# Gate and up: product 7 of two units as seven half-size products in three groups between the products of the next pair

## The chip, the cores and the metric

One core of a Trainium2 chip runs the whole kernel. The metric is the device time of one execution in microseconds (us), as the median of several runs. A measurement of this kernel is compared with the kernel before on the same chip. The engines are named as in the profile: PE (TensorE, matmuls), PEld (its weight loads), DVE (VectorE), ACT (ScalarE), POOL (GpSimd) and SP (SyncE, which issues DMAs).

## The reference

An encoder trunk of two layers on 1024 tokens of width 1024, in float32. The change concerns the first half of the channel mixer of each layer, the gate-and-up product:

```python
D_FF = 2816
h = rmsnorm(x, norm_ffn[i])
gu = h @ w_gate_up[i]                       # (1024, 1024) @ (1024, 5632)
x = x + (jax.nn.silu(gu[..., :D_FF]) * gu[..., D_FF:]) @ w_down[i]
```

The rest (two kinds of attention, memory heads, output projection, down projection, norms) is as it was.

## The kernel before

A float32 product is made of three fp32r matmuls: each operand is split into a high part (`hi`, L106, a cast on ACT) and a low part (`lo`, L109, a subtraction on DVE), and `three` gives high x high, high x low and low x high, which add up in one bank of PSUM.

Gate and up runs over 22 units a layer (class `Pair`, one for 128 columns of the gate and the 128 of up that belong to them; here the word pair means two such units in a row, u and v, and the pair behind it w and x). The tokens are two halves of 512, and rows of the weights are two halves of 512 too, so that a unit is a 2x2 block product. It is done with seven products instead of eight. Product n (0 to 6) takes a left tile, a sum of blocks of the weight, and a right tile `B[n]`, a sum of blocks of the normalized tokens, kept for the whole layer. A product is 12 matmuls of 128x512 (4 row blocks by 3 terms, L886). Products 0, 2, 4 and 6 go into bank X of the unit (units take turns between two banks), 1, 3 and 5 into Y.

`prepare` makes the left tiles of two products at a time. Products 0 and 1 use the raw weight as loaded; products 2 and 3 use a sum and a difference that POOL forms in the tile `wS` (L848, L841), products 4 and 5 two more differences that POOL writes over the same `wS`; product 6 uses half of the raw tile. The split tiles are `wgu2` for 2 and 3 (one buffer), `wgu6` for 6 (one buffer), `wgu` for the others (three buffers). A `prepare` is called four products ahead (`lead`), and the ones for products 4 and 6 each start the next load of a raw tile (L937, on SP).

`read` takes the results out: ACT copies (L897 to L909), DVE adds and multiplies (L894), ACT does silu (L900, L915). Product 6 is read by DVE as `c1 -= X` and `c1 *= g1`. After product 6 of the second unit, `hand_over` (L1012) makes from the four results of two units the right tiles of the down projection and stores them (L1006).

The order on PE is the order of `product` calls, unit by unit, except that the first four units (`first`) run two by two, while `right_sides` makes the `B` tiles for them step by step on DVE and ACT (L975, L978). The order on the other engines comes from a scheduler, as engines follow the program and the tiles' buffers. At the end of a layer's list the first tiles of the down projection are made ready (L1058 on), and its products follow (L1178).

Of the kernel before, what the change touches and what calls it, by code (L numbers as in the profile page):

```python
# [41 lines left out]
def trunk_kernel(ctx: ExitStack, tc: tile.TileContext, a: dict, out: bass.AP):  # L42
# [62 lines left out]
    def hi(dst, src):  # L105
        nc.scalar.copy(dst, src)  # L106

    def lo(dst, src, h, eng=None):
        (eng or nc.vector).tensor_tensor(dst, src, h.bitcast(F32), op=ALU.subtract)  # L109
# [74 lines left out]
    class Norm:  # L184
# [6 lines left out]
        def add(self, xk, k=None):  # L191

            n = self.n
            self.xs[len(self.xs) if k is None else k] = xk
            sq = temp("sq", n)
            nc.scalar.activation(sq, xk, AF.Square)
            if len(self.xs) > self.summed:
                while self.acc:
                    self.mean(self.acc.pop(0))
                self.mean(sq)  # L200
                return
            self.acc.append(sq)
            if len(self.xs) > 2:
                self.merge()
# [66 lines left out]
    with tc.tile_pool(name="mp", bufs=1, reuse_waits="tile") as mp:  # L271
# [94 lines left out]
    for layer in range(2):  # L366
# [427 lines left out]
        with (  # L794
            tc.tile_pool(name=f"fs{layer}", bufs=1, reuse_waits="tile") as fs,
            tc.tile_pool(name=f"fp{layer}", bufs=1, reuse_waits="tile") as fp,
        ):
            phase[:] = fp, 21, 5
            wide[:] = True, 2

            def pair(src, dst):
# [17 lines left out]
            norms = [Norm(), Norm()]  # L819

            B = [[None] * 4 for _ in range(7)]
            def load_x(m, f):
                x[m][f] = temp("x")
                nc.sync.dma_start(x[m][f], (a["x"] if is_a else x_d)[m][:, f * HS : (f + 1) * HS])

            class Pair:
# [6 lines left out]
                def prepare(self, n):  # L833

                    n -= n % 2
                    if n in self.left:
                        return
                    g1, g2 = self.raw[0][:, :HS], self.raw[0][:, HS:]
                    if n > 0:
                        u1, u2 = self.raw[1][:, :HS], self.raw[1][:, HS:]  # L840
                    sub = lambda o, p_, q_: nc.gpsimd.tensor_tensor(o, p_, q_, op=ALU.subtract)  # L841
                    s = self.raw[0]
                    if n == 2:
                        self.s = fs.tile([P, D], F32, tag="S", name="wS", bufs=2)
                    if n in (2, 4):
                        s = self.s
                    if n == 2:
                        nc.gpsimd.tensor_tensor(s[:, HS:], u1, u2, op=ALU.add)  # L848
# [12 lines left out]
                    if n == 6:  # L861
                        hi(w[:, 0, :HS], u2)
                        lo(w[:, 1, :HS], u2, w[:, 0, :HS])
                    else:
                        hi(w[:, 0], s)
                        lo(w[:, 1], s, w[:, 0])
                    self.left[n], self.left[n + 1] = w[:, :, :HS], w[:, :, HS:]
                    if n == 4:
                        self.left[4], self.left[5] = self.left[5], self.left[4]
                    if n > 3 or (n == 0 and 2 <= self.j < first):  # L870
                        load_gu()

                def product(self, n):
                    if n == 0:
                        self.X = (
                            ps_s.tile([P, HS], F32, tag="S", name="X")
                            if self.j % 2
                            else ps_mm.tile([P, HS], F32, tag="mm", name="X")
                        )
                    if n in (1, 3):  # L880
                        self.Y = ps_t.tile([P, HS], F32, tag="T", name="Y")
                    ps, w = (self.Y if n in (1, 3, 5) else self.X), self.left[n]
                    for k in range(4):
                        kw = (w[:, 0, k * P : (k + 1) * P], w[:, 1, k * P : (k + 1) * P])
                        for i, (l, r) in enumerate(three(kw, (B[n][k][:, 0], B[n][k][:, 1]))):
                            nc.tensor.matmul(  # L886
                                ps, l, r, start=n in (0, 1, 3, 6) and k == 0 and i == 0,
                                stop=k == 3 and i == 2, skip_group_check=True,
                            )

                def read(self, n):
                    self.seen.add(n)
                    X, Y = self.X, getattr(self, "Y", None)
                    add = lambda o, p_, q_, op=ALU.add: nc.vector.tensor_tensor(o, p_, q_, op=op)  # L894
                    if n == 0:
                        self.g1 = temp("g1")
                        nc.scalar.copy(self.g1, X)  # L897
                    elif n == 1:
                        add(self.g1, Y, self.g1)
                        nc.scalar.activation(self.g1, self.g1, AF.Silu)  # L900
                    elif n == 2:
                        self.g2 = temp("g2")
                        nc.scalar.copy(self.g2, X)  # L903
                    elif n == 3:
                        self.c2 = temp("c2")
                        nc.scalar.copy(self.c2, Y)  # L906
                    elif n == 4:
                        self.c1 = temp("c1")
                        nc.scalar.copy(self.c1, X)  # L909
                        add(self.c2, self.c2, self.c1)  # L910
                        if 5 in self.seen:
                            add(self.c2, self.c2, self.g2, ALU.mult)
                    elif n == 5:
                        add(self.g2, Y, self.g2)
                        nc.scalar.activation(self.g2, self.g2, AF.Silu)  # L915
# [9 lines left out]
            for j in range(0, first, 2):  # L925
                order += [(u, n) for n in (3, 2, 5, 4, 6) for u in us[j : j + 2]]
# [45 lines left out]
            def right_sides():  # L972
# [24 lines left out]
                for k in range(4):  # L997
                    sub(x[k][1], x[k + 4][1], x[k][1])
                    B[4][k] = pair(x[k][1], h_op(k))
                    yield  # L1000
                for k in range(4):
                    B[6][k] = pair(x[k + 4][0], t_op(k))
                    yield

            def keep(i, p, t):
# [26 lines left out]
            def gate_up():  # L1032
                run_some(rest, 1)
                load_gu()
                for i, (u, n) in enumerate(order):
                    if i + lead < len(order):
                        v, n_ = order[i + lead]
                        v.prepare(n_)
                    u.product(n)
# [4 lines left out]
                    yield u, n  # L1044


            wd = a["w_dn"][layer].rearrange("(p i) r c -> p i r c", i=2)
# [162 lines left out]
            for u, n in gate_up():  # L1210
                if u.j == NF - 1 and n in (2, 3, 4):
                    keep_rows(n - 2)
                    if n > 2:
                        left_side(0, n - 3)
                if u.j == NF - 1 and n in (3, 4, 5):
                    right_side(0, n - 3)
# [127 lines left out]
```

## Time and profile before

| | |
|---|---|
| runs shown | 2156.21, 2150.68, 2151.85 us; median 2151.85 |
| profiled execution | 2155.14 us, span 2153.4 us, mean granted TensorE clock 0.992 |
| matmuls of gate and up | L886, three groups X<-hB, X<-hT and Y<-hB of 1056 with 254.2, 254.2 and 257.0 us busy, and smaller ones |
| POOL, DVE and ACT in the gate-and-up | some 13, 23 and 14 us of every 38.16 us |

In a row of the timeline the first number is the start in us, the second the busy time, then engine, line, operation, output<-inputs by the program's names, shape and count, and in brackets the idle time in front with what ended it. In a row of groups the numbers behind the bar are the busy time in all (us) and the mean of one (ns). In a row of windows the busy time of each engine stands in a stretch, the granted clock of PE (1.00 is full), the share of the DMA engines and GB/s.

### The profile page before, as it was taken

Reading aid. Unit: us, or ns where it says so; the run is one execution under the profiler, and the core shown is the slowest. Engines: PE = TensorE matmul, PEld = TensorE weight load, DVE = VectorE, ACT = ScalarE, POOL = GpSimd, SP = SyncE. Lnnn points to the kernel's source line nnn. Section 1 sums busy time; section 2 is a strip of 40 time slices with the busy share of each in tenths; the row PEclk is TensorE's granted clock in tenths of the full one; section 3 lists DMA queues with packets and bytes.
Section 4 is the critical chain, followed back from the end, with each engine's and each line's share of the span. In section 5 each row is a group of like instructions: output and inputs, shape, how many; then the busy total and the mean of one; then the engine's idle time right before and its main releaser. Section 6 shows DMA issues by size and latency. Waiting matters only on the chain.

```text
span 2153.4 us, 27952 instructions
## 1 busy us (share of the span) xinstructions
PE 2111.0 (98%) x9946; PEld 1744.3 (81%) x9946; DVE 1458.7 (68%) x2314; ACT 1045.2 (49%) x1988; POOL 509.5 (24%) x545
## 2 busy tenths in 40 slices
PE   7999999999999999999999999999999999999997
PEld 6788888778888888888778888887888888888886
DVE  7677787786556565866766666667866665567675
ACT  6577785443333334344466665653433333344442
POOL 0344330333333330000233233203233333300000
PEclk9999999999999999999999999999999999999998
DMA  6321118333323336865332212275133323277662
GB/s 247 100 93 44 37 60 287 124 91 100 113 94 117 98 118 225 298 215 201 105 91 66 78 58 72 86 246 168 58 119 117 98 93 113 93 247 261 203 208 93
DMA packets 120076, 287.22 MB, mean 133 GB/s; under 512 B 12288, under 2 KB 18688, under 8 KB 119936
## 3 DMA queue, kind: packets, MB, share of 16 engines
q1 hardware_dynamic: 112896, 272.57, 38.5%
q10 hardware_dynamic: 7040, 12.85, 1.6%
q8 instruction: 79, 1.29, 0.2%
q14 instruction: 61, 0.50, 0.1%
HBM read 210.40 MB, written 68.94 MB: 130 GB/s over the span
## 4 chain that ended last, share of the span: by engine, by line
PE 75%; issue 13%; DVE 4%; ACT 3%; DMA 2%; POOL 2%; DVEq 0%; SPq 0%; ACTq 0%; POOLq 0%
PE X L886 20%; PE Y L886 16%; PE mm L139 14%; PE po L139 6%; PE X L1178 5%; PE Y L1178 4%; PE S L559 3%; PE O L622 3%; PE pT L602 3%; DMA xr_d<-x 1%; DMA x<-in_x 1%; ACT p L574 1%; POOL wS L841 1%; DVE wgu L109 1%; DVE pl L109 0%
## 5 line engine op out<-in xcount | busy, mean ns | idle before, releaser
L109 DVE TENSOR_TENSOR wgu<-wS,wgu 128x1024 fp32r<-128x1024 f32 x88 | 111.0, 1261 | 255.9 <-ACT wgu L106 255.9
L886 PE MATMUL Y<-hB,wgu 128*128 128x512 f32 x1056 | 257.0, 393 | 0.8 <-ACT c L906 0.8
L886 PE MATMUL X<-hB,wgu 128*128 128x512 f32 x1056 | 254.2, 390 | 1.0 <-ACT g L903 1.0
L886 PE MATMUL X<-hT,wgu 128*128 128x512 f32 x1056 | 254.2, 391 | 0.0
L1178 PE MATMUL X<-hB,wd 128*128 128x512 f32 x1056 | 242.4, 390 | 0.9 <-DVE x L1146 0.9
L886 PEld LDWEIGHTS Y<-hB,wgu 128*128 128x128 f32 x1056 | 198.5, 188 | 44.7 <-ACT c L906 1.6
L886 PEld LDWEIGHTS X<-hB,wgu 128*128 128x128 f32 x1056 | 198.4, 188 | 43.9 <-ACT g L903 1.9
L886 PEld LDWEIGHTS X<-hT,wgu 128*128 128x128 f32 x1056 | 198.5, 188 | 42.8
L1178 PEld LDWEIGHTS X<-hB,wd 128*128 128x128 f32 x1056 | 198.0, 188 | 43.1 <-issue 2.3
L587 POOL TENSOR_SCALAR p<-p,stat 128x384 f32<-128x384 f32 (+1 forms) x256 | 141.0, 570 | 313.2 <-DVE stat L584 212.8
L139 PE MATMUL mm<-hT,wqk 128*128 128x512 f32 x672 | 199.9, 405 | 0.1
L139 PE MATMUL po<-yT,wo 128*128 128x512 f32 x768 | 184.7, 394 | 0.0
L1178 PE MATMUL Y<-hB,wd 128*128 128x512 f32 x792 | 180.4, 389 | 0.0
L1178 PEld LDWEIGHTS Y<-hB,wd 128*128 128x128 f32 x792 | 148.5, 188 | 31.2 <-DVE x L1146 0.5
L139 PEld LDWEIGHTS po<-yT,wo 128*128 128x128 f32 x768 | 142.5, 188 | 29.5 <-issue 1.0
L106 ACT CAST wgu<-wS 128x1024 fp32r<-128x1024 f32 x88 | 92.4, 1050 | 131.3 <-POOL wS L841 108.1
L233 POOL TENSOR_TENSOR nr<-nv,neg_half 128x4 f32<-128x4 f32 (+1 forms) x11 | 11.7, 1063 | 598.5 <-DVE nv L232 598.4
L841 POOL TENSOR_TENSOR wS<-wgu_raw 128x512 f32<-128x512 f32 x44 | 65.9, 1498 | 362.9 <-DVE wgu L109 362.9
L106 ACT CAST hB<-b_raw 128x512 fp32r<-128x512 f32 x154 | 89.4, 618 | 112.0 <-DMA b_raw<-b_d 96.0
L574 ACT ACTIVATE p<-p,stat 128x256 f32<-128x256 f32 (+1 forms) x192 | 112.3, 586 | 52.2 <-DVE stat L570 49.5
L109 DVE TENSOR_TENSOR pl<-pT,ph 128x384 fp32r<-128x384 f32 (+1 forms) x256 | 118.7, 494 | 21.8 <-ACT ph L106 18.8
L109 DVE TENSOR_TENSOR hB<-b_raw,hB 128x512 fp32r<-128x512 f32 x154 | 99.8, 686 | 49.5 <-ACT hB L106 49.3
(161 smaller groups left out, 3924.6 us busy)
## 6 DMA issues: line engine op xcount, KB each, us to landing
wgu_raw<-in_w_gu SPq DMA_DIRECT2D x92, 512.0 KB
wd_raw<-in_w_dn SPq DMA_DIRECT2D x70, 512.0 KB
b_raw<-b_d SPq DMA_DIRECT2D x70, 512.0 KB
b_d<-c SPq DMA_DIRECT2D x88, 256.0 KB
b_d<-t SPq DMA_DIRECT2D x66, 256.0 KB
wo_raw<-in_w_out SPq DMA_DIRECT2D x32, 512.0 KB
x<-in_x SPq DMA_DIRECT2D x32, 256.0 KB
xr_d<-x ACTq DMA_DIRECT2D x32, 256.0 KB
```

The costliest lines, as they stand in the source:

```text
L106: nc.scalar.copy(dst, src)
L109: (eng or nc.vector).tensor_tensor(dst, src, h.bitcast(F32), op=ALU.subtract)
L139: nc.tensor.matmul(ps[:, :n], l, r, start=start and i == 0 and j == 0, stop=stop and i == len(order) - 1 and j == 2,)
L233: nc.gpsimd.tensor_tensor(r[:, :nb], v[:, :nb], neg_half[:, :nb], op=ALU.pow)
L559: nc.tensor.matmul(s_[:, :n], Q[self.h][:, qb * P : (qb + 1) * P], k, start=j == 0, stop=j == 1)
L574: nc.scalar.activation(p[:, :n], p[:, :n], AF.Exp, bias=m1, scale=-1.0, accum_out=s1)
L587: nc.gpsimd.tensor_scalar(p[:, :n], p[:, :n], ri[:, i : i + 1], 1.0, op0=ALU.mult, op1=ALU.mult)
L602: nc.tensor.transpose(tr[:, j * P : (j + 1) * P], p[:, j * P : (j + 1) * P], ident)
L622: nc.tensor.matmul(o[:, c0 : c0 + w * P], self.value(j), t[:, s0 : s0 + w].rearrange("p j q -> p (j q)"), start=j == js[0] and t is self.p ...
L841: sub = lambda o, p_, q_: nc.gpsimd.tensor_tensor(o, p_, q_, op=ALU.subtract)
L886: nc.tensor.matmul(ps, l, r, start=n in (0, 1, 3, 6) and k == 0 and i == 0, stop=k == 3 and i == 2, skip_group_check=True,)
L1178: nc.tensor.matmul(bank, l, r, start=i in (0, 1, 3, 6) and p == 0 and n == 0, stop=p == HF - 1 and n == 2, skip_group_check=True,)
```

## The change

Product 7 of a unit (n = 6) is no longer made in the unit. A new class `Fourth` takes it for two units together: the left side is then 2x2 blocks of half the rows and half the columns, and so is the right side, and it is done with seven products of 6 matmuls of 128x256 (42 in place of 24 of 128x512). The result is added into or taken from `c1` of the two units directly. The seven products come in three groups: A (two, 12 matmuls), B (two, 12) and C (three, 18). They stand between the products of the next pair: A, w0, B, w1, C, w2 and so on; for the last pair of a layer they follow at the end. In the first pair's case (`skip`) A, B and C stand after (u2,3), (u3,3).

- Left tiles: `prepare` of group A makes all of them. POOL forms a sum and three differences of 128x256 in a tile `wS4` (L933, L932), ACT and DVE split into four high and four low parts, `wgu4`, in tiles of 2 KB a partition, of which there are now 24 in place of 21. The tile `wgu6` is gone, and so are product 7's own `hi` and `lo`. Both of the loads that product 6 started are started here.
- Right tiles: three new ones, t2, t3 and t4 (`q4h`), formed in `right_sides` by eight DVE operations of 128x256 with three `hi` and three `lo`.
- Banks: X4 and Y4, one each for all three groups. The reads (L985) are seven DVE operations and two products for a pair; A's are two of 128x256, B's two, C's three.
- `hand_over` comes after C.
- `ahead` is the list in which `prepare` is called; the last units' hooks into the down projection now count items from the end.

```diff
-                    elif n == 6 and self.j >= first:
-                        w = fp.tile([P, 2, HS], F32R, tag="w4", name="wgu6", bufs=1)
...
+                def prepare(self, n):
...
+                    nc.gpsimd.tensor_tensor(s1, r1[:, :h2], r1[:, h2:], op=ALU.add)
+                    sub(s2, s1, r0[:, :h2])
+                    sub(s3, r0[:, :h2], r1[:, :h2])
+                    sub(s4, r0[:, h2:], s2)
...
+                def product(self, n):
...
+                    if n == "A":
+                        self.X = ps_t.tile([P, HS], F32, tag="T", name="X4")
+                        self.Y = ps_o.tile([P, HS], F32, tag="O", name="Y4")
+                        self.part(self.X, 0, a11, b11, start=True)
+                        self.part(self.Y, 0, a12, b21, start=True)
+                    elif n == "B":
+                        self.part(self.X, 0, s2, t2)
+                        self.part(self.Y, h2, s1, t1)
                     else:
-                        add(self.c1, self.c1, X, ALU.subtract)
-                        add(self.c1, self.c1, self.g1, ALU.mult)
+                        self.part(self.X, 0, s3, t3)
+                        self.part(self.Y, h2, s4, b22, stop=True)
+                        self.part(self.X, h2, a22, t4, stop=True)
+
+                def read(self, n):
...
+                    if n == "A":
+                        sub(a.c1[:, low], X[:, low])
+                        sub(a.c1[:, low], Y[:, low])
+                    elif n == "B":
+                        sub(a.c1[:, high], X[:, low])
+                        sub(b.c1[:, high], Y[:, high])
+                    else:
+                        sub(
+                            b.c1.rearrange("p (n c) -> p n c", n=2),
+                            X[:, low].unsqueeze(1).to_broadcast([P, 2, h2]),
+                        )
+                        sub(a.c1[:, high], Y[:, high])
+                        sub(b.c1[:, low], X[:, high], ALU.add)
+                        for u in self.units:
+                            sub(u.c1, u.g1, ALU.mult)
...
-            order += [(u, n) for u in us[first:] for n in range(7)]
+            ahead, before = list(order), []
+            for j in range(0, NF, 2):
...
+                z = Fourth(us[j], us[j + 1])
+                parts4 = [(z, n) for n in "ABC"]
+                ahead += own + parts4[:1]
+
+                skip = 2 if j == 2 else 0
+                order += own[:skip]
+                for i, it in enumerate(own[skip:]):
+                    order += before[i : i + 1] + [it]
+                before = parts4
+            order += before
...
-                    if n == 6 and u.j % 2:
-                        hand_over(u.j // 2, us[u.j - 1], u)
+                    if n == "C":
+                        hand_over(u.units[0].j // 2, *u.units)
```

DVE at the end of a unit in the middle of layer 0, before the change; the unit is v, the names with 6007, 6010 and 6044 are the next unit's (w's) tiles for products 2 to 5, raw_5820 belongs to the unit after it (x).

```order
L109 TENSOR_TENSOR wgu2_6010<-wS_6007,wgu2_6010 128x1024
L894 TENSOR_TENSOR c2_5990<-c2_5990,c1_6004 128x512
L109 TENSOR_TENSOR wgu_6044<-wS_6007,wgu_6044 128x1024
L894 TENSOR_TENSOR g2_5972<-Y_5977,g2_5972 128x512
L109 TENSOR_TENSOR wgu_6098<-wgu_raw_5820,wgu_6098 128x1024
L894 TENSOR_TENSOR c2_5990<-c2_5990,g2_5972 128x512
L894 TENSOR_TENSOR c1_6004<-c1_6004,X_5925 128x512
L109 TENSOR_TENSOR wgu6_6079<-wgu_raw_5785,wgu6_6079 128x512
L894 TENSOR_TENSOR c1_6004<-c1_6004,g1_5938 128x512
```

The same place after the change; c1_5922 is u's and c1_6045 is v's, X4 and Y4 are the banks of the two units' `Fourth`.

```order
L109 TENSOR_TENSOR wgu2_6051<-wS_6048,wgu2_6051 128x1024
L889 TENSOR_TENSOR c2_6031<-c2_6031,c1_6045 128x512
L109 TENSOR_TENSOR wgu_6087<-wS_6048,wgu_6087 128x1024
L889 TENSOR_TENSOR g2_6013<-Y_6018,g2_6013 128x512
L985 TENSOR_TENSOR c1_5922<-c1_5922,X4_6069 128x256
L109 TENSOR_TENSOR wgu_6173<-wgu_raw_5945,wgu_6173 128x1024
L889 TENSOR_TENSOR c2_6031<-c2_6031,g2_6013 128x512
L985 TENSOR_TENSOR c1_5922<-c1_5922,Y4_6070 128x256
L985 TENSOR_TENSOR c1_5922<-c1_5922,X4_6069 128x256
L985 TENSOR_TENSOR c1_6045<-c1_6045,Y4_6070 128x256
```

The first five positions are the same but for the lines' numbers; A's reads of X4 and Y4 stand where, or one place ahead of where, the read of product 6 stood, and B's follow.

PE behind v5, the last product of v, after the change (w0's four rows shown by the first and last; Y_6018 is v's bank, X_6092 w's). Before, product 6 of v stood there (two rows of 6 matmuls into X_5925, 128x512), and w0 behind it.

```order
L881 MATMUL Y_6018<-hB_4758,wgu_5942 128x512 x3
L957 MATMUL X4_6069<-hT8_4854,wgu4_5982 128x256 x2
L957 MATMUL X4_6069<-hT8_4854,wgu4_5983 128x256
L957 MATMUL X4_6069<-hT8_4854,wgu4_5982 128x256 x2
L957 MATMUL X4_6069<-hT8_4854,wgu4_5983 128x256
L957 MATMUL Y4_6070<-hT8_4879,wgu4_5982 128x256 x2
...
L881 MATMUL X_6092<-hB_4210,wgu_6015 128x512 x3
...
L881 MATMUL X_6092<-hB_4339,wgu_6015 128x512 x3
L957 MATMUL X4_6069<-q4h_4906,wgu4_5989 128x256
...
L957 MATMUL Y4_6070<-hT8_4854,wgu4_5989 128x256 x2
```

Group B goes into the banks X4 and Y4 that group A filled, one product of w later.

POOL at the same place after the change; wS_6048 is w's and wS_6205 x's.

```order
L849 TENSOR_TENSOR wS_6048<-wgu_raw_5789 128x512
L842 TENSOR_TENSOR wS_6048<-wS_6048,wgu_raw_5698 128x512
L849 TENSOR_TENSOR wS_6205<-wgu_raw_5997 128x512
L842 TENSOR_TENSOR wS_6205<-wS_6205,wgu_raw_5945 128x512
L842 TENSOR_TENSOR wS_6048<-wgu_raw_5698,wgu_raw_5789 128x512
L842 TENSOR_TENSOR wS_6048<-wgu_raw_5698,wS_6048 128x512
L933 TENSOR_TENSOR wS4_6278<-wgu_raw_5997 128x256
L932 TENSOR_TENSOR wS4_6278<-wgu_raw_5789,wgu_raw_5997 128x256
```

The order of the `wS` operations is that of before (x's first two ahead of w's last two); the four of `wS4` are new behind them, and the raw tile of x is loaded by the `prepare` of the pair's group A rather than by those of products 4 and 6 alone.

More of the change, by code (lines that the diff above doesn't have):

```diff
@@ L821, in trunk_kernel @@
             B = [[None] * 4 for _ in range(7)]
+            fourth = []
             def load_x(m, f):
@@ L886, in product @@
                             nc.tensor.matmul(
-                                ps, l, r, start=n in (0, 1, 3, 6) and k == 0 and i == 0,
+                                ps, l, r, start=n in (0, 1, 3) and k == 0 and i == 0,
                                 stop=k == 3 and i == 2, skip_group_check=True,
@@ L924, in trunk_kernel @@
             order = [(u, n) for u in us[:first] for n in (0, 1)]
-            for j in range(0, first, 2):
-                order += [(u, n) for n in (3, 2, 5, 4, 6) for u in us[j : j + 2]]
-            order += [(u, n) for u in us[first:] for n in range(7)]
+            ahead, before = list(order), []
+            for j in range(0, NF, 2):
+                if j < first:
+                    own = [(u, n) for n in (3, 2, 5, 4) for u in us[j : j + 2]]
+                else:
+                    own = [(u, n) for u in us[j : j + 2] for n in range(6)]
+                z = Fourth(us[j], us[j + 1])
[7 more added lines that the diff above has]
+            order += before
             loads = [(us[j], 0) for j in range(first)] + [(us[0], 1), (us[1], 1)]
@@ L1000, in right_sides @@
                     yield
+                t2, t3, t4 = (temp("q4").rearrange("p (k c) -> p k c", k=2) for _ in range(3))
+                for k in range(2):
+                    top, bottom = x[k + 4][0], x[k + 6][0]
+                    sub(t3[:, k], bottom[:, h2:], top[:, h2:])
+                    sub(top[:, h2:], top[:, h2:], top[:, :h2])
+                    sub(t2[:, k], bottom[:, h2:], top[:, h2:])
+                    sub(t4[:, k], t2[:, k], bottom[:, :h2])
+                    yield
                 for k in range(4):
                     B[6][k] = pair(x[k + 4][0], t_op(k))
+                    yield
+                for t in (t2, t3, t4):
+                    f = [fp.tile([P, 2, h2], F32R, tag="t2k", name="q4h", bufs=24) for _ in range(2)]
+                    hi(f[0], t)
+                    lo(f[1], t, f[0])
+                    fourth.append(f)
                     yield
@@ L1034, in gate_up @@
                 load_gu()
+                ready = lead
                 for i, (u, n) in enumerate(order):
-                    if i + lead < len(order):
-                        v, n_ = order[i + lead]
+                    while n in range(6) and ready < min(ahead.index((u, n)) + lead + 1, len(ahead)):
+                        v, n_ = ahead[ready]
                         v.prepare(n_)
+                        ready += 1
                     u.product(n)
@@ L1041, in gate_up @@
                     run_some(rest, 1 if i < 2 * first else 2)
-                    if n == 6 and u.j % 2:
-                        hand_over(u.j // 2, us[u.j - 1], u)
-                    yield u, n
+                    if n == "C":
+                        hand_over(u.units[0].j // 2, *u.units)
+                    yield i - len(order)
             wd = a["w_dn"][layer].rearrange("(p i) r c -> p i r c", i=2)
@@ L1208, in finish @@
                     nc.scalar.dma_start(out[:2].rearrange("k p t -> p k t")[:, :, at:], first)
[L1210 to L1216, printed above, removed]
+            for to_go in gate_up():
+                if -7 <= to_go <= -5:
+                    keep_rows(to_go + 7)
+                    if to_go > -7:
+                        left_side(0, to_go + 6)
+                if -6 <= to_go <= -4:
+                    right_side(0, to_go + 6)
             norms = [Norm(), Norm() if is_a else Norm(HS, 7)]
```

53 lines of the change are left out of this document (46 added, 7 removed).

## The prediction

> **What bounds the kernel now.** I read the page first, for the share of each engine over the whole span, and then went to the gate-and-up stage by stretches.
>
> ```profile
> span 2153.4 us, 27952 instructions
> PE 2111.0 (98%) x9946; PEld 1744.3 (81%) x9946; DVE 1458.7 (68%) x2314; ACT 1045.2 (49%) x1988; POOL 509.5 (24%) x545
> ```
>
> PE is the bound: all idle time that it has is 42 us. The profiled run took 2155.14 us, of which 1.7 lie outside the span. That is 3.3 us above the median of the runs shown (2151.85); the sum below is made against 2155.14 and shifted by 3.3 at the end. The next view is the busy time in stretches of 38.16 us, in layer 0.
>
> ```profile
> core 0: us, PE busy (x) PEld busy (x) DVE busy (x) ACT busy (x) POOL busy (x), PEclk, DMA share, GB/s
> 597.60:635.76 38.16, 38.16 (x169) 31.57 (x169) 23.13 (x24) 14.04 (x20) 12.77 (x8) 1.00 0.31 104
> ```
>
> A pair of units is 14 products of 12 matmuls: 168 matmuls in 38.16 us, 227.1 ns each, 2.73 a product. PE has no idle time here and the others have much. Every pair that the change alters is therefore bound by PE, unless it gives PE a new wait. What stands between them is a chain of other engines that runs once a unit. Here it is at the end of a unit, in the timelines of PE, DVE and POOL.
>
> ```profile
> start us, us, engine line op out<-in xcount [idle before <-releaser]
> 619.24 2.89 PE L886 MATMUL X<-hB,wgu 128*128 128x512 f32 x12
> 621.97 2.89 PE L886 MATMUL Y<-hB,wgu 128*128 128x512 f32 x12
> 624.69 2.89 PE L886 MATMUL X<-hT,wgu 128*128 128x512 f32 x12
> 627.42 2.89 PE L886 MATMUL X<-hB,wgu 128*128 128x512 f32 x12
> ...
> 621.01 1.23 DVE L109 TENSOR_TENSOR wgu<-wS,wgu 128x1024 fp32r<-128x1024 f32 x1 [3.81 <-ACT wgu L106]
> ...
> 626.42 1.22 DVE L109 TENSOR_TENSOR wgu<-wS,wgu 128x1024 fp32r<-128x1024 f32 x1 [2.26 <-ACT wgu L106]
> 627.56 0.68 DVE L894 TENSOR_TENSOR g<-Y,g 128x512 f32<-128x512 f32 x1
> 628.16 1.22 DVE L109 TENSOR_TENSOR wgu<-wgu_raw,wgu 128x1024 fp32r<-128x1024 f32 x1
> 629.30 1.78 DVE L894 TENSOR_TENSOR c<-c,g 128x512 f32<-128x512 f32 x1
> 631.00 0.68 DVE L894 TENSOR_TENSOR c<-c,X 128x512 f32<-128x512 f32 x1
> ...
> 622.32 1.30 POOL L841 TENSOR_TENSOR wS<-wgu_raw 128x512 f32<-128x512 f32 x1 [8.79 <-DVE wgu L109]
> 623.56 1.74 POOL L841 TENSOR_TENSOR wS<-wgu_raw,wS 128x512 f32<-128x512 f32 x1
> ```
>
> Call t0 the start of the unit's product 4 on PE (619.24). The next unit's left tile wgu2 has one buffer, so its first part waits for product 3 to end, at t0. From there one thing follows the other: the low part on DVE (t0+1.8 to +3.0), two subtractions on POOL over the same tile (+3.1 to +6.1), a cast, and the low part of the next unit's tile for products 4 and 5 (+7.2). Behind it, in DVE's order, stand the add of g2, the low part for the unit after next, the product with g2, and only then the read of product 6, at +11.8. Product 6 had left PE by +8.3, so the read comes 3.4 us late; nothing waits for it, since the next unit's product 0 has another bank. The waits view says that the chain is no accident of one unit:
>
> ```profile
> POOL wS L841 <- DVE wgu L109: 362.9, 44, 15.8
> DVE wgu L109 <- ACT wgu L106: 275.7, 90, 6.1
> ```
>
> **The change, part by part.** *Fewer columns on PE.* Per pair 24 matmuls of 512 columns go and 42 of 256 come. The kernel already has matmuls of this width elsewhere:
>
> ```profile
> 42.77 1.95 PE L139 MATMUL mm<-mhl,wm 128*128 128x256 f32 x15
> L139 PE MATMUL mm<-mhl,wm 128*128 128x256 f32 x15 | 1.9, 281 | 0.0
> ```
>
> Fifteen take 1.95 us with the last one's 0.281, so they start (1.95 - 0.28)/14 = 0.119 us apart. Removed 24 x 0.2271 = 5.45, added 42 x 0.119 = 5.00: 0.45 us less a pair, 22 pairs in two layers, **10.0 us less**. The most that this part could give, at half the wide matmul's pace (0.1136), is 0.68 a pair or 15 us.
>
> [...]
>
> *Reads that PE now waits for.* This is the term that decides the sign. The products of a group go into two banks, X4 and Y4, which the groups A, B and C share. Group B adds into columns that A's read must have left, so B's matmuls wait for A's reads on DVE. On PE after the pair's last product (v5) stand A, the next unit's product 0, and B. Unstalled, counted from t0: v4 to +2.73, v5 to +5.45, A (12 x 0.119 = 1.43) to +6.88, product 0 to +9.61, B's X half (0.71) to +10.32, where B's Y half wants A's second read.
>
> On DVE the second read stands in the same place of the chain that the read of product 6 had: behind the low part of the next w4, the add of g2, A's first read, the low part of x0 and the product with g2. From the rows: w4's low part at +7.18, the add of g2 at +8.32 until about +8.92, A's first read 0.38 until +9.30, the low part 1.14 until +10.44, the product with g2 0.60 to 1.70, and the second read 0.38. The 0.38 is from this group, a quarter the size from PSUM:
>
> ```profile
> 1090.95 0.75 DVE L109 TENSOR_TENSOR V<-vtr,V 128x256 fp32r<-128x256 f32 x2
> L894 DVE TENSOR_TENSOR c<-c,g 128x512 f32<-128x512 f32 x31 | 36.5, 1176 | 0.7 <-ACT g L915 0.7
> L894 DVE TENSOR_TENSOR g<-Y,g 128x512 f32<-128x512 f32 x31 | 21.1, 682 | 0.0
> ```
>
> The c, g product takes 1176 on the mean, 1.78 where POOL runs beside it; undisturbed it should be near the 0.60 from the start of g2's add to the next start (627.56 to 628.16). So the second read ends at +11.4 at best and +12.5 as the chain ran in before: PE waits **1.1 to 2.2 us** at each boundary of two pairs.
>
> There is one more thing ahead in the chain. In the changed program POOL has the two subtractions of the unit after next (x2) in front of those for w4; in before they are in front too, but early. They need a raw tile whose load is now issued later, since the raw tile before it is also read for Fourth's left tiles, whose low parts lie some 6 us before t0 on DVE. A load's way to POOL is in these waits:
>
> ```profile
> 629.03 1.50 POOL L848 TENSOR_TENSOR wS<-wgu_raw 128x512 f32<-128x512 f32 x1 [3.72 <-DMA wgu_raw<-in_w_gu]
> 630.61 1.62 POOL L841 TENSOR_TENSOR wS<-wS,wgu_raw 128x512 f32<-128x512 f32 x1
> ```
>
> With an issue near t0-3.5 and 3.6 us to landing, the two (3.1 us together) run from about t0 to t0+2 on, and end at +3.2 to +5.2, against the +3.1 at which w4's subtractions began. That puts the chain back by 0.1 to 2.1 us. The bounds are thus 1.1 and 2.2 + 2.1 = 4.3 (4.8 with a first read that is late too); I take the middle of the delay, **3.3 us**. The boundaries with the whole chain are those behind pairs 2 to 9, 8 a layer and 16 in all: 16 x 3.3 = **+52.8 us**. Group C is free of this: between B and it lies product 1 (2.73 us), and three reads of 0.38 fit into that.
>
> *Early stage.* For the first four units product 6 of two units is gone from where it stood as 24 matmuls, so (u2,3) and (u3,3) come 5.45 us earlier, while DVE has eight more operations of 256 and three low parts to make for Fourth's right tiles.
>
> ```profile
> 460.00:470.00 10.00, 10.00 (x44) 8.05 (x43) 8.84 (x9) 3.78 (x5) 6.38 (x4) 1.00 0.52 155
> 459.80 5.75 PE L886 MATMUL X<-hT,wgu 128*128 128x512 f32 x24
> 461.16 1.22 DVE L109 TENSOR_TENSOR wgu<-wS,wgu 128x1024 fp32r<-128x1024 f32 x1 [1.21 <-ACT wgu L106]
> 464.62 2.31 DVE L109 TENSOR_TENSOR wgu<-wS,wgu 128x1024 fp32r<-128x1024 f32 x1
> ```
>
> The two low parts end at 462.4 and 466.9 in before. They would be wanted at 459.8 and 462.5, so PE could wait up to 4.4 us; with three reads less ahead of them I take 2.5 a layer, **+5.0**, with 0 and 7 a layer as ends.
>
> *The rest of the added work* (per pair four POOL operations of 256, four casts and four low parts less the two of product 7, three small reads more) is some 3 us on POOL, 1 on ACT and 2 on DVE of 38.16, beside the 25, 24 and 15 us that they idle in the stretch above: nothing, as long as it isn't in the chain. At the end of each layer A, B and C of the last pair stand among the first down-projections, and I put **+1** for both (ends 0 and 4).
>
> Sum: 2155.14 - 10.0 + 52.8 + 5.0 + 1.0 = 2203.9; against the median, 3.3 lower, **2201 us**.
>
> **The rivals.** *The wait doesn't come.* If DVE has the product with g2 and the low part of x0 done by t0+9.9, A's second read ends by +10.3, PE never waits, and only the narrower products remain: 2151.85 - 10 = 2142 us, faster. For it speaks that DVE is idle 15 us of 38; against it, that the idle time lies in front of the chain, not behind it: to decide, the chain must be 1.1 us shorter than the best that the rows allow.
>
> *A small wait.* The x2 subtractions run before t0 as they did, and POOL leaves DVE alone: 16 x 1.1 = 18, less 10, early 0 to 5: 2160 to 2165.
>
> *The clock falls too.* This happened once in layer 0 (the four last rows; the first is for comparison):
>
> ```profile
> 470.00:480.00 10.00, 9.62 (x42) 7.48 (x42) 9.31 (x8) 4.92 (x8) 5.73 (x5) 1.00 0.59 184
> ...
> 414.00:416.00 2.00, 1.10 (x7) 0.59 (x5) 1.66 (x2) 0.45 (x1) 1.92 (x2) 1.00 0.45 174
> 416.00:418.00 2.00, 2.00 (x12) 1.77 (x13) 0.16 (x1) 0.00 (x0) 1.67 (x2) 0.77 0.00 0
> 418.00:420.00 2.00, 2.00 (x6) 1.06 (x5) 0.69 (x1) 0.00 (x0) 0.17 (x1) 0.50 0.00 0
> 420.00:422.00 2.00, 2.00 (x8) 1.43 (x7) 1.13 (x2) 0.00 (x0) 0.00 (x0) 0.88 0.00 0
> ```
>
> After 0.90 us of idle PE the granted clock was 0.77, 0.50 and 0.88 for 2 us each: 0.46 + 1.00 + 0.24 = 1.7 us lost. A wait of 3.3 at 16 places could lose up to 16 x 1.7 = 27 more: 2228. Against it: the 0.38 us that PE idled between 470 and 480 left the clock at 1.00, so not every gap does it.
>
> [...]
>
> *Weights bound the narrow matmuls.* Each matmul has its own weight load:
>
> ```profile
> L886 PEld LDWEIGHTS X<-hB,wgu 128*128 128x128 f32 x1056 | 198.4, 188 | 43.9 <-ACT g L903 1.9
> ```
>
> If 188 ns were the pace, 42 x 0.188 = 7.9 in place of 5.0: 2.9 us a pair, 64 us in all where no wait covers it. That would be 2206 even without the DVE wait. Against it stand the 15 matmuls at 0.119, with loads of their own.
>
> **How the numbers follow.** The wait behind the chain, between 2180 and 2236: 0.74, of which 0.10 with dips of the clock on top. A small wait, 2157 to 2180: 0.15. No wait, about 2142: 0.09. The loads as the pace are 0.02, and land in the first case's range. The low end of the range is 1.1 at each boundary with 1 or 2 for the early stage, 2162; the high end 4.8 at each (76.8), 14 early and 4 at the end, less 10: 2151.85 + 84.8 = 2236. Outside are the no-wait case and some dips. Since about 0.3% (6.5 us) is what a measurement can tell from no change, faster is 0.09, the same 0.05 (the low part of the small wait), slower 0.86.
>
> **What would show it.** In the changed profile the busy stretch of a pair should be about 41 us with PE idle 2 to 4 us in one piece, in front of the Y4 matmuls of group B, released by DVE's Y4 read; that read at t0+12 to +14; POOL's w4 subtractions at t0+3.2 to +5.2. Starts of 256-column matmuls 0.119 apart confirm the saving. If PE has no idle time between pairs, the chain was misjudged; if PE's idle time is in front of product 0 or of group A, it is another wait than I named.

## The result and the profile after

The changed kernel takes 2248.0 us at the median against 2151.2 for the one before: 1.0448 times as long, 95% interval 1.0426 to 1.0470. The forecast was 2201, with a range to 2236. Slower was right; the size was not. One execution of the changed kernel (5751.68 us), and below one each of e4 (7408.82) and e5 (2991.16), took far longer than its others and is in no ratio; the other five of the changed kernel have a median of 2246.87.

The profiled execution of the changed kernel took 2245.84 us. Its page begins so (us busy, share of the span, instructions):

```profile
span 2244.1 us, 29148 instructions
PE 2140.9 (95%) x10342; PEld 1772.6 (79%) x10342; DVE 1523.5 (68%) x2490; ACT 1060.2 (47%) x2038; POOL 604.7 (27%) x633
```

The span grew by 90.7 us. PE was idle 42.4 us before and 103.2 now, 60.8 more; and it was busy 29.9 us more, though its matmuls are 10 us less work. So there are two losses, and only the first is a wait. The waits view of PE (engine, line, what it waited for: us in all, times, longest) names the first:

```profile
PE Y L957 <- DVE c L985: 34.2, 16, 2.1
PE X L957 <- DVE c L985: 20.4, 21, 4.6
...
PE Y L881 <- ACT wgu L106: 4.8, 2, 2.5
...
PE Y L881 <- DVE wgu L109: 1.9, 2, 1.0
```

Both rows of L957 are group B, which waits for A's reads: 54.6 us. The two others are the early stage. The timelines of PE, DVE and POOL at the end of a pair show the wait itself:

```profile
570.57 3.02 PE L881 MATMUL X<-hB,wgu 128*128 128x512 f32 x12
...
577.59 2.90 PE L881 MATMUL X<-hB,wgu 128*128 128x512 f32 x12
580.88 0.98 PE L957 MATMUL X<-q4h,wgu 128*128 128x256 f32 x6 [0.39 <-DVE c L985]
584.00 1.65 PE L957 MATMUL Y<-hT,wgu 128*128 128x256 f32 x6 [2.14 <-DVE c L985]
585.45 3.58 PE L881 MATMUL Y<-hB,wgu 128*128 128x512 f32 x12
588.87 0.88 PE L957 MATMUL X<-q4h,wgu 128*128 128x256 f32 x6
589.58 0.88 PE L957 MATMUL Y<-hT,wgu 128*128 128x256 f32 x6
...
578.67 1.23 DVE L109 TENSOR_TENSOR wgu<-wS,wgu 128x1024 fp32r<-128x1024 f32 x1 [3.52 <-ACT wgu L106]
579.82 0.69 DVE L889 TENSOR_TENSOR g<-Y,g 128x512 f32<-128x512 f32 x1
580.42 0.41 DVE L985 TENSOR_TENSOR c<-c,X 128x256 f32<-128x256 f32 x1
580.75 1.74 DVE L109 TENSOR_TENSOR wgu<-wgu_raw,wgu 128x1024 fp32r<-128x1024 f32 x1
582.41 1.21 DVE L889 TENSOR_TENSOR c<-c,g 128x512 f32<-128x512 f32 x1
583.54 0.41 DVE L985 TENSOR_TENSOR c<-c,Y 128x256 f32<-128x256 f32 x1
...
571.08 1.30 POOL L849 TENSOR_TENSOR wS<-wgu_raw 128x512 f32<-128x512 f32 x1 [4.99 <-DMA wgu_raw<-in_w_gu]
...
574.58 1.74 POOL L842 TENSOR_TENSOR wS<-wgu_raw 128x512 f32<-128x512 f32 x1
```

Here t0 is 570.57. Unstalled, B's Y half would have started at t0+10.32, 580.89; it started at 584.00, 3.1 late. The chain is the one of the prediction: the next unit but one's subtractions on POOL first (t0+0.5, when their raw tile landed), w4's only at t0+4.0, w4's low part at t0+8.1, and A's second read at t0+13.0. At the next two boundaries the same difference is 3.5 and 3.0.

The second loss stands right behind. The first matmuls after the gap take 1.65 us where six of the same shape take 0.88 at 589.58, and product 1 of the next unit 3.58 in place of 2.9. The windows view of these microseconds gives the granted clock in the third column from the end:

```profile
580.00:582.00 2.00, 1.47 (x9) 0.84 (x7) 2.00 (x3) 1.11 (x2) 2.00 (x3) 1.00 0.25 102
582.00:584.00 2.00, 0.00 (x0) 0.00 (x0) 2.00 (x4) 0.00 (x0) 1.92 (x2) 0.86 0.00 0
584.00:586.00 2.00, 2.00 (x8) 1.90 (x9) 0.59 (x2) 0.00 (x0) 0.20 (x1) 0.50 0.38 139
586.00:588.00 2.00, 2.00 (x9) 1.59 (x8) 0.11 (x1) 0.00 (x0) 0.00 (x0) 0.78 0.00 0
588.00:590.00 2.00, 2.00 (x15) 1.84 (x14) 0.69 (x1) 0.15 (x1) 0.00 (x0) 1.00 0.00 0
```

Half the clock, for 3.4 us from 583.45 on; such a stretch is called a dip below. Read in stretches of 1 us, 14 of the 16 full boundaries show one, and it lasts 3.4 us or twice that (three of them). The mean granted clock over the span tells the sum: 0.979 now and 0.992 before, so 2140.9 x 0.021 = 45 against 2111.0 x 0.008 = 17, **28 us** of full-speed work lost. Read in stretches of 0.5 us, the dips at the boundaries alone lose 27.0; the early stages lose 5.4 against 1.7 before, and the first 400 us, which the change doesn't touch, 4.8 less than before.

### The profile page after: what moved, and what is told of

Its sections match the earlier page's. It is cut to its first block, busy times and chain, and to the rows that moved or that the text cites. A ratio compares the mean times of both kernels' runs of the same rounds, so it can differ in the third digit from the quotient of the medians.

```text
span 2244.1 us, 29148 instructions
## 1 busy us (share of the span) xinstructions
PE 2140.9 (95%) x10342; PEld 1772.6 (79%) x10342; DVE 1523.5 (68%) x2490; ACT 1060.2 (47%) x2038; POOL 604.7 (27%) x633
## 4 chain that ended last, share of the span: by engine, by line
PE 32%; issue 5%; DVE 5%; POOL 4%; ACT 2%; DMA 2%; DVEq 0%; POOLq 0%; SPq 0%; ACTq 0%
PE mm L139 8%; PE X L1288 4%; PE Y L1288 4%; PE po L139 4%; PE Y L881 3%; POOL wS L842 3%; PE X L881 2%; PE S L559 2%; PE O L622 2%; DMA wgu_raw<-in_w_gu 2%; DVE wgu L109 1%; PE pT L602 1%; DVE c L889 1%; POOL wS L932 1%; ACT wgu L106 1%
## 5 line engine op out<-in xcount | busy, mean ns | idle before, releaser
L881 PE MATMUL Y<-hB,wgu 128*128 128x512 f32 x1056 | 276.0, 414 | 0.0
L109 DVE TENSOR_TENSOR wgu<-wS,wgu 128x1024 fp32r<-128x1024 f32 (+1 forms) x132 | 140.7, 1079 | 197.6 <-ACT wgu L106 197.6
L881 PEld LDWEIGHTS Y<-hB,wgu 128*128 128x128 f32 x1056 | 212.4, 203 | 46.7 <-issue 1.0
L106 ACT CAST wgu<-wS 128x1024 fp32r<-128x1024 f32 (+1 forms) x132 | 117.6, 906 | 141.3 <-POOL wS L842 126.1
L881 PE MATMUL Y<-hT,wgu 128*128 128x512 f32 x528 | 129.5, 394 | 6.8 <-ACT wgu L106 4.8
L109 DVE TENSOR_TENSOR pl<-pT,ph 128x384 fp32r<-128x384 f32 (+1 forms) x256 | 118.7, 494 | 20.7 <-ACT ph L106 17.6
L881 PE MATMUL X<-hT,wgu 128*128 128x512 f32 x528 | 127.6, 391 | 0.0
L895 ACT ACTIVATE g<-g 128x512 f32<-128x512 f32 x44 | 27.8, 632 | 211.0 <-DVE g L889 211.0
```

Source lines behind the costliest of these rows:

```text
L881: nc.tensor.matmul(ps, l, r, start=n in (0, 1, 3) and k == 0 and i == 0, stop=k == 3 and i == 2, skip_group_check=True,)
```

## The experiments

Theory 1: PE's gap of 0.5 and 2.1 us, which DVE's order of reads makes, costs itself, and makes the clock fall behind it. Theory 2: the clock falls for something in the narrow matmuls, and the gap is beside the point. Each kernel ran beside the one before on the same chip.

| run | median us | ratio to before (95%) |
|---|---|---|
| e1_fill12 | 2222.17 | 1.0318 (1.0303 to 1.0334) |
| e2_fill6 | 2229.44 | 1.0352 (1.0324 to 1.0380) |
| e3_space | 2178.76 | 1.0118 (1.0103 to 1.0133) |
| e4_bank | 2180.02 | 1.0121 (1.0104 to 1.0138) |
| e5_onebank | 2198.26 | 1.0204 (1.0186 to 1.0223) |
| e6_both_skip1 | 2167.95 | 1.0070 (1.0055 to 1.0085) |
| e7_both_skip0 | 2170.28 | 1.0078 (1.0063 to 1.0093) |
| e8_skip1_silu | 2167.82 | 1.0068 (1.0051 to 1.0085) |
| e9_raw6 | 2164.06 | 1.0051 (1.0036 to 1.0066) |
| e10_latet | 2169.26 | 1.0077 (1.0062 to 1.0092) |
| e11_latet_raw6 | 2166.36 | 1.0061 (1.0044 to 1.0078) |
| e12_copy_first | 2155.37 | 1.0008 (0.9999 to 1.0017) |

### The gap filled with useless work (e1, e2)

```diff
+                    if n == "B" and order[i - 1][1] == 0:
+                        order[i - 1][0].fill(12)
...
+                def fill(self, count):
...
+                    self.Y = ps_t.tile([P, HS], F32, tag="T", name="Y")
...
+                    for i in range(count):
...
+                        nc.tensor.matmul(
+                            self.Y, w[:, 0, k * P : (k + 1) * P], B[0][k][:, 0], start=i == 0,
...
```

> The changed kernel with 12 useless matmuls of 512 columns in front of every group B that follows product 0 of a unit (into that unit's Y bank, which product 1 starts anew), so that PE works 2.7 us of the 3.1 us that it waits there. Theory 1 (the gap makes the clock fall): idle time in front of the narrow matmuls falls from 54.6 us to about 10 to 15, the granted clock goes from 0.979 to 0.99 or more, and though the wait is as long as before the time falls by the some 32 us of half clock, to 2210 to 2222. Theory 2 (the narrow matmuls, not the gap, make the clock fall): clock near 0.979, and 2243 to 2255.

> The same with 6 useless matmuls, so that one gap of some 1.7 to 1.9 us is left of 0.5 and 2.1. Theory 1 with a threshold near 2 us of idle time: as with twelve, 2210 to 2222. Theory 1 with any gap of a microsecond or more: most dips stay, 2235 to 2250. Theory 2: 2243 to 2255.

With twelve, the clock is 0.990 and the kernel some 26 us faster than the changed one, at the very end of theory 1's range, though PE does 12 matmuls more at each place. The waits left in front of the narrow matmuls are these:

```profile
PE X L969 <- DVE c L997: 5.9, 4, 1.8
...
PE Y L969 <- DVE c L997: 4.0, 11, 0.6
```

Theory 2 is out: the narrow matmuls are all there, and between 530 and 900 us no microsecond has a granted clock under 0.95. With six, the time lies between the cases that were set down: one gap of 1.35 to 1.80 us is left at each of the 16 places; two have a dip behind them, and the time varied from run to run more than with twelve (2222 to 2233). The two sorts, first without and then with a dip, in PE's timeline and in windows behind it:

```profile
708.63 0.98 PE L969 MATMUL Y<-hT,wgu 128*128 128x256 f32 x6 [1.57 <-DVE c L997]
...
710.00:712.00 2.00, 2.00 (x11) 1.64 (x10) 0.07 (x1) 0.00 (x0) 0.00 (x0) 1.00 0.00 0
...
750.10 0.98 PE L969 MATMUL Y<-hT,wgu 128*128 128x256 f32 x6 [1.75 <-DVE c L997]
...
752.00:754.00 2.00, 2.00 (x6) 1.60 (x5) 0.00 (x0) 0.00 (x0) 0.00 (x0) 0.50 0.00 0
```

### The same gap with wide matmuls only, in the kernel before (e5)

```diff
                         self.X = (
+                            ps_o.tile([P, HS], F32, tag="O", name="X")
+                            if self.j > first and self.j % 4 in (1, 2)
+                            else ps_s.tile([P, HS], F32, tag="S", name="X")
```

> The kernel before, without the change, but at four places a layer a unit and the next share one X bank, so PE waits there for the late read of product 6: by the rows of before from t0+8.2 to about t0+12.5, 4.2 us of idle time at 8 places, all matmuls 512 wide. Theory 1 (a gap of more than about 2 us halves the clock, whatever the matmuls are): every one of these places has a stretch of granted clock 0.5 behind it, some 1.7 to 3.4 us lost each; idle time +33, clock 0.98 to 0.985, time 2195 to 2215. Theory 2 (only narrow matmuls do it): clock 0.992 as before, 2180 to 2190.

PE waits 3.36 us as listed at each of the 8 places, 26.8 us in all, somewhat less than the 4.2 worked out. Seven of the eight have a dip, and the time lies in theory 1's range; the clock, 0.988, is a little above the 0.985 that it allowed. The gap without a dip, and one with, in PE's timeline, and the windows behind the second:

```profile
615.84 3.06 PE L888 MATMUL X<-hB,wgu 128*128 128x512 f32 x12 [3.36 <-DVE c L896]
...
695.86 4.61 PE L888 MATMUL X<-hB,wgu 128*128 128x512 f32 x12 [3.36 <-DVE c L896]
...
696.00:698.00 2.00, 2.00 (x6) 1.54 (x7) 1.97 (x3) 0.00 (x0) 0.34 (x1) 0.54 0.50 139
698.00:700.00 2.00, 2.00 (x7) 1.58 (x6) 1.41 (x3) 0.00 (x0) 0.00 (x0) 0.61 0.79 199
```

The matmuls are all 512 wide here, so the gap alone is enough. But two gaps of the same 3.36 us came out differently: whether a gap is punished isn't settled by its length alone. Here are stretches of 3.41 us, the length of a dip, first around two boundaries of the changed kernel, both with a last gap of 2.14 us, then around e5's gap without a dip. Their edges lie whole lengths of a dip from the start of a dip in the same trace:

```profile
580.04:583.45 3.41, 1.43 (x9) 0.80 (x7) 3.41 (x4) 1.11 (x2) 3.33 (x4) 1.00 0.15 59
583.45:586.86 3.41, 2.86 (x10) 2.57 (x11) 1.25 (x4) 0.00 (x0) 0.75 (x1) 0.50 0.22 82
...
1713.26:1716.67 3.41, 2.18 (x12) 1.44 (x10) 3.41 (x5) 1.34 (x3) 2.79 (x3) 1.00 0.30 119
1716.67:1720.09 3.42, 2.18 (x12) 1.95 (x13) 1.93 (x4) 0.00 (x0) 1.35 (x2) 1.00 0.20 77
1720.09:1723.50 3.41, 3.41 (x24) 3.15 (x23) 1.08 (x2) 0.63 (x1) 0.00 (x0) 1.00 0.00 0
...
610.81:614.23 3.42, 1.68 (x8) 1.05 (x6) 3.42 (x4) 1.81 (x3) 1.07 (x1) 1.00 0.38 144
614.23:617.64 3.41, 1.80 (x8) 1.48 (x9) 3.38 (x5) 0.00 (x0) 2.01 (x2) 1.00 0.20 77
617.64:621.05 3.41, 3.41 (x17) 2.80 (x16) 2.21 (x4) 0.59 (x1) 0.00 (x0) 1.00 0.81 229
```

At the first boundary one stretch has most of the idle time, with PE busy for 1.43 us of it, and the clock in the next was 0.50. At the other two places the idle time is split over two stretches, with PE busy for 2.18 and 2.18 us and for 1.68 and 1.80, and the clock stayed at 1.00. These are three places; no run moved a gap and left its length as it was, so what decides isn't shown.

### Two ways to take the wait away (e3, e4)

```diff
-                    order += before[i : i + 1] + [it]
+                    at = i if j < 2 * 2 else {0: 0, 2: 1, 3: 2}.get(i, 3)
+                    order += before[at : at + 1] + [it]
```

```diff
+                        self.Y2 = ps_mm.tile([P, HS], F32, tag="mm", name="Y4b")
+                        self.part(self.Y2, h2, s1, t1, start=True)
                         self.part(self.X, 0, s2, t2)
-                        self.part(self.Y, h2, s1, t1)
...
```

> Groups further apart in the steady part: A, w0, w1, B, w2, C, so product 1 (2.7 us) lies beside A's reads. If the wait for A's reads and the dips behind it are the loss: PE's idle time in front of narrow matmuls falls from 54.6 to 5 to 15 us, the clock to 0.99, and 2158 to 2172 (the first two pairs' waits, some 17 us, mostly stay, the 10 us of narrower work are gained). If the narrow matmuls slow PE or the clock by themselves: 2190 or more. If the wait only moves to C: 2200 or more.

> Groups where they are, but B's and C's high half of Y4 in a bank of its own (Y4b), and B begins with it, so only A's first read is waited for, which ends near t0+10.3, when PE is at t0+10.3 too. If the second read's wait (2.1 us at 16 places) is the main loss: idle time in front of narrow matmuls 10 to 20 us, few dips, 2162 to 2180. If it only moves to group C (whose reads of B then are late): 2200 or more.

Either one takes 68 to 69 us off. In e4 the Y row is gone from the waits and the X row is `9.2, 7, 3.7`, its largest piece, 3.7, at the second pair in layer 0. So the wait was for A's second read, and it didn't move to group C. But both stop 27 us above before, e3 some 7 above what was expected and e4 at the upper end of it. In e4's windows of one pair each, layer 0, PE has no idle time and full clock, and still a pair takes longer than the 38.16 of before:

```profile
643.30:681.59 38.29, 38.28 (x186) 31.91 (x186) 24.64 (x31) 14.65 (x22) 17.05 (x12) 1.00 0.30 102
```

The 0.45 us a pair that the narrower matmuls give is used up by something smaller than a listed wait, and the rest of the 27 us is early in the layers: in e4's layer 0, 6.6 us of listed waits (2.44, 0.47 and 3.69) and some 5 of half clock.

### The early stage (e6, e7, e9, e10, e11)

All have e3's and e4's edits together. e6 and e7 set `skip` to 1 and 0; e9 gives one more raw tile (`phase[:] = fp, 22, 6`); e10 forms t2 and t4 behind the B[6] tiles with `skip` 1; e11 is e10 with e9's tile.

> Both remedies (groups further apart, own bank for B) and, early in the layer, A and B of the first pair one and two products sooner, so that 1.4 us of them lie beside the wait for u3's left tile. If the 27 us by which the two remedies alone are slower than before are the early waits (some 2.9 us of gap and 3.4 us of lost clock there, 3.7 and 1.7 at the second pair, each layer): 2150 to 2162. If these waits aren't it: 2170 or more.

> As e6 with the first pair's groups sooner by one product more: A ahead of (u2,3), B and C behind it. If the right tiles q4h are ready by then, 2150 to 2160; if PE now waits for them instead, 2160 to 2180.

> Both remedies with six raw tiles in place of five (and 22 tiles of 2 KB in place of 24). Fourth holds the raw tiles of u0 and u1 longer, so u3's raw tile is loaded late early in the layer (POOL waits 7.6 us for it in e4's trace), and PE waits for u3's left tile. If the load is the cause: the early wait of 2.4 + 0.5 us with its 3.4 us of lost clock goes in each layer, and the time is 2155 to 2168, 10 or more below e3 and e4. If DVE's order is the cause: within 4 us of 2175.

> e6 with four of the eight operations of 256 for the new right tiles (t2, t4) behind the B[6] tiles on DVE. In e6 group A waits 5.3 us in each layer for a B[6] tile. If DVE's added work ahead of those tiles is the cause: that wait falls to 2 us or less, and the time by 7 to 12 us, to 2155 to 2162. If B[6] is late for another reason: within 4 us of e6's 2168.

> e9 and e10 together, the shortest that these remedies give: if the sum holds (narrower matmuls -10, ACT and DVE hiccups +5, the rest hidden) 2146 to 2156, that is within 0.3% of before. If the early stage stays DVE's: 2160 to 2170.

e6 is 11 us faster than e3 and still 6 us above its range, and e7 is where its second case put it: put sooner, group A waits for its own right tile (5.3 us a layer in e6, `PE Y L957 <- DVE hT L109`), which DVE makes late, and the clock falls there too (in e6 to 0.50 in each stretch of 1 us from 466 to 472). e10 takes that wait away, and in its place 4.6 and 3.0 us of a wait for A's reads come up behind it; the time is that of e6. That points to DVE's work as a whole, which no run made lighter here; DVE was busy 9.2, 6.4, 8.8 and 9.3 us of the four stretches of 10 us from 440 on in before. e9 is within its range: with a sixth raw tile the wait for u3's left tile on ACT falls from 2.4 (e4) to 0.45 us in each layer, and of the early dips one is left, in layer 0. No run joins the two remedies with the old `skip` and five raw tiles, so the share of the sixth tile in e9's time isn't separated from theirs. e11 came out in its second case, with the same wait as e10.

### What eats the narrow matmuls' gain (e8, e12)

```diff
                         add(self.g1, Y, self.g1)
-                        nc.scalar.activation(self.g1, self.g1, AF.Silu)
...
-                        nc.scalar.copy(self.g2, X)
+                        copied = nc.scalar.copy(self.g2, X)
...
+                        with tc.issue_after(copied.ins):
+                            nc.scalar.activation(self.g1, self.g1, AF.Silu)
```

(e12's; the first four units keep the old order.)

> e6 with the silu of g1 behind the copy of g2 on ACT. In the two remedies' traces product 4 starts 0.17 us late and its first matmuls are 0.14 us longer, since g2's copy stands behind that silu, which waits for DVE. If that costs 0.3 us a unit that carries Fourth's left tiles, 16 to 18 in all: 4 to 6 us less than e6. If it is something of the weights or the clock: no difference.

> e9 with the copy of g2 held ahead of the silu of g1 on ACT from the fifth unit on (in e8 the scheduler kept the old order, so e8 didn't test it). In e9 PE waits for that copy 16 times, 0.2 us each as listed and some 0.3 with the longer first matmuls. If that is what eats the narrower matmuls' gain in the steady part: the row PE X L881 <- ACT g goes, a pair takes 37.9 to 38.0 us in place of 38.3, and the time falls by 4 to 6 us from 2164, to 2158 to 2160. If product 4 is late for another reason: 2162 to 2166.

e8 moved the silu in the text only; in its trace ACT still runs it ahead of the copy, so it tests nothing. In e12 the copy is first. It is the run that settles the point; ACT (the two first rows) and PE in e9, then ACT and one pair's window in e12:

```profile
677.15 0.63 ACT L895 ACTIVATE g<-g 128x512 f32<-128x512 f32 x1 [3.35 <-DVE g L889]
677.69 0.57 ACT L898 COPY g<-X 128x512 f32<-128x512 f32 x1
675.21 2.88 PE L881 MATMUL Y<-hT,wgu 128*128 128x512 f32 x12
678.31 3.02 PE L881 MATMUL X<-hB,wgu 128*128 128x512 f32 x12 [0.22 <-ACT g L898]
681.17 2.89 PE L881 MATMUL Y<-hB,wgu 128*128 128x512 f32 x12
```

```profile
672.13 0.59 ACT L899 COPY g<-X 128x512 f32<-128x512 f32 x1 [1.60 <-PE X L881]
673.86 0.63 ACT L902 ACTIVATE g<-g 128x512 f32<-128x512 f32 x1 [1.14 <-DVE g L889]
...
642.32:680.10 37.78, 37.78 (x187) 32.08 (x186) 25.47 (x31) 14.79 (x22) 16.21 (x13) 1.00 0.31 105
```

In e9 the silu waits for DVE, where the four new low parts of Fourth's left tiles stand ahead of g1's add; the copy behind the silu ends at 678.26, and product 4, which adds into the bank that the copy empties, starts then. In e12 a pair takes 37.78 us, 0.38 less than before and 0.51 less than e9's 38.29. The listed wait was 0.22; the rest stands in the rows of PE in e9. Products follow each other at 2.72 to 2.73 us there, though each is listed with 2.88, so a product without a wait starts before the listed end of the one in front. Product 4 starts 3.10 behind product 3, 0.38 late, and product 5 another 2.86 behind it, 0.13 late: 0.51. The time fell by 9 us, not by the 4 to 6 expected, because I had counted 0.3 a pair and not 0.5.

e12 is at 1.0008, with 1 inside the interval: no version beat the kernel before. The 0.38 us a pair is spent again, and what the trace shows to have taken it is what is left of the early waits (2.2, 1.0, 0.7, 0.5 and 0.5 us in layer 0, and one dip).

## Why the prediction was wrong

**The mechanism was right.** The wait that was named (group B, for A's Y4 read on DVE, behind w4's low part, x0's low part and the product with g2) is where PE idles, and e4 shows it by taking away just that wait. Its size was right too: 3.3 us a boundary forecast, 3.1, 3.5 and 3.0 at three of them, 16 places. POOL's delay by x2's subtractions was put at 0.1 to 2.1 us and was 0.9. One premise held in part only: that group B adds into columns that A's read must have left. In X4 it does; in Y4 B writes the upper half (`self.part(self.Y, h2, ...)`) and A's read takes the lower (`Y[:, low]`), so what they share is the bank. Whether they could go side by side in one bank, no run shows.

**The step that failed is the rival on the clock**, which had a chance of 0.10, against it the sentence that not every gap does it, and no place in the sum or the range. That rested on one gap of 0.38 us without a dip, a ninth of the gap that the forecast itself put at every boundary; the larger of the two gaps that it looked at, 0.90 us, did have its dip. A wait of 3.3 us should have carried the dip as its likeliest companion. It did at 14 of 16 places, and cost 28 us by the mean clock. The 27 that the rival had priced came out in part by luck: it put 1.7 us at 16 places, where 14 came and three of them lasted twice as long. e1 and e5 show that the gap, not the narrow matmuls, is its cause: gap filled, the mean clock is back at 0.990; gap without narrow matmuls, the clock falls to 0.50 at 7 of 8 places. Why it was nearly every time, and not at the other 2 of 16 here and 1 of 8 in e5, isn't shown.

**The early stage was mis-sized**: 2.5 us a layer forecast (0 to 7), measured 9.0 and 8.1 us of listed waits. The largest is one that I had put at nothing, the boundary behind the second pair:

```profile
497.32 1.62 PE L957 MATMUL X<-q4h,wgu 128*128 128x256 f32 x6 [4.63 <-DVE c L985]
...
491.13 3.45 DVE L889 TENSOR_TENSOR c<-c,c 128x512 f32<-128x512 f32 x2
494.51 2.33 DVE L889 TENSOR_TENSOR c<-c,g 128x512 f32<-128x512 f32 x2
496.76 0.41 DVE L985 TENSOR_TENSOR c<-c,X 128x256 f32<-128x256 f32 x1
```

There two units end at once, so DVE has four operations of 1.2 to 1.7 us ahead of A's first read, beside POOL's.

**The saving was right in its own place and hidden elsewhere.** 256-column matmuls start 0.119 us apart (588.87 to 589.58 for six), as forecast. But the new low parts, costed at nothing since DVE has 15 us free, push g1's add back and through ACT's order product 4, 0.3 us a pair in the changed kernel (products 3, 4 and 5 start at 610.11, 613.00 and 615.86, 5.75 us where two products take 5.45) and 0.5 in e9.

The terms now: -10 for the narrower matmuls, 16 x 3.2 = 51 for the wait, 17 for the early stage, about 5 for product 4, 28 for the clock: 91, where the spans have 90.7. That they meet so closely is chance: the clock's term is good to some 2 us. The forecast's sum had 49; the clock's 28, 12 of early waits and product 4's 5 are the difference, less 3 for the smaller terms.

What stays open: what decides whether a gap has a dip behind it, why some dips last 6.8 us in place of 3.4, and by how much the early stage could still be mended with a lighter load on DVE.

## What to carry to other kernels

Where PE runs without a gap, a new gap has two prices: its own length and the half clock behind it. In these traces the second came behind 14 of 16 gaps of 2.1 us and 7 of 8 of 3.36 us, and behind 2 of 16 of 1.35 to 1.80 us, each time with 3.4 us or twice that at a clock of 0.50. So count both for gaps like the longer ones, and look in the trace for the dip behind each gap that is there already. A read that nobody waited for gets a price as soon as its bank is used again in the same breath; give the second use another bank, or put one more product between (PE waited 34.2 us in front of Y4 here, and with a bank of its own in e4 that row was gone). And a trace that lists no wait can still lose a few tenths at each short wait (0.51 us in e9, with 0.22 listed): compare the period of a loop, not only the list of waits.

## What the runs showed of the hardware

- Gaps of PE of 2.1 us (after another of 0.3 to 0.8) were followed by a granted clock of 0.50 at 14 of 16 places, gaps of 1.35 to 1.80 us at 2 of 16, gaps of 3.36 us at 7 of 8; the low clock lasted 3.4 us or twice that.
- Of two gaps of 2.14 us in the changed kernel (ahead of the matmuls at 584.00 and 1717.91), and of two of 3.36 us in e5 (695.86 and 615.84), the first had a granted clock of 0.50 behind it and the second 1.00.
- A listed wait of 0.22 us in front of a product of 12 matmuls (e9) cost 0.51 us of the loop's period (38.29 against 37.78 in e12).
